# SwiGLU gate and up projections as seven Strassen block products, with SBUF regions by phase

## The chip, the cores and the metric

One core of one Trainium2 chip runs the kernel. The metric is device time in microseconds (us) for one call. The engines are TensorE (PE, with its weight loads PEld), VectorE (DVE), ScalarE (ACT), GpSimd (POOL) and SyncE (SP, which only issues DMAs here).

## The reference

One decoder layer over 512 tokens of 1024 features, in float32. Two feed-forward blocks (FFNs, width 2816) stand around a mixer; a gated per-layer embedding (PLE) and a final norm follow:

```python
def swiglu(x, w_gate, w_up, w_down):
    return (jax.nn.silu(x @ w_gate) * (x @ w_up)) @ w_down
...
    h = h + 0.5 * swiglu(rmsnorm(h, ffn1_norm[i]), ffn1_w_gate[i], ffn1_w_up[i], ffn1_w_down[i])
    n = rmsnorm(h, mix_norm[i])
    proj = n @ w_in[i]
    ...
    h = h + jnp.concatenate([ya, yb], axis=-1) @ w_out[i]
    h = h + 0.5 * swiglu(rmsnorm(h, ffn2_norm[i]), ffn2_w_gate[i], ffn2_w_up[i], ffn2_w_down[i])
    gate = jax.nn.sigmoid(rmsnorm(h, ple_norm[i]) @ ple_w_gate[i] + ple_b_gate[i])
    h = h + gate * (p[i] @ ple_w_proj[i])
return rmsnorm(h, final_norm)
```

## The kernel before

Activations lie in SBUF with features on the 128 partitions and the 512 tokens along the free axis. A weight unit is 128 x 1024: 128 output features, eight contraction tiles. Every float32 product is three float32r passes (`passes`, L151 to L153): weights and activations are each split into a rounded part `hi` and a rest `lo`, and hi*hi + hi*lo + lo*hi accumulate in PSUM. A unit is loaded by SP (`raw`, four buffers), its `hi` is written by ACT (L121, tile `whi`, three buffers) and its `lo` by DVE (L122, `wlo`, three buffers). So a unit costs 24 matmuls of 128 x 512, one ACT cast and one DVE subtraction.

An FFN (`swiglu`) goes through its 22 tiles of width in parts of 8, 7 and 7. In each part every tile has one gate unit and one up unit (48 matmuls). Its results are multiplied by the token's norm factor `r` on DVE, silu on ACT, the product on POOL (L252), and the split for the next projection by ACT (L135) and POOL (L136). Then eight down units, one for each of eight feature tiles of `h`, accumulate that part, and DVE adds them to `h` (L275). After the last part, tile by tile, ACT and DVE make the operand of the next stage (`scaled_split`, L143, L144), and ACT and POOL add the squares for the next norm (L193, L194). The norm's factor commutes with a projection and is worked out behind the first products.

At the start the tiles of `x` and quarter units of the first two weights arrive in turn, and the first products follow tile by tile. The PLE projection (`emb`, L718 to L726, 48 matmuls from `p`) stands between the mixer's output projection and FFN2.

All tiles come from one SBUF pool with a number of buffers for each tag. A scheduler in the language's tile layer sets the order on each engine when the kernel is built; every engine then works through its own list in order, and waits where a row's operands or buffers are not ready.

## Time and profile before

| what | value |
|---|---|
| time, median of 3 runs | 1152.52 us (1152.34 to 1154.45) |
| profiled execution, first to last instruction | 1151.7 us; beside that span no other time of it is recorded, and the median lies 0.8 us above it |
| PE busy | 1134.0 us, 98% of the span |
| DVE, ACT, POOL busy | 605.6, 418.2, 255.2 us |
| granted TensorE clock | 0.998 on the mean |
| gate and up units of both FFNs | 88 units, 2112 matmuls of 128 x 512 |

"Busy" of PE is the union of overlapping matmuls, so the spacing of their starts, not their duration, says what one costs. In a row of a group the numbers behind the bar are busy us and mean ns of one instruction, then the idle time just before it and what ended it.

### The profile page before, as it was taken

Reading aid. Unit: us, or ns where it says so; the run is one execution under the profiler, and the core shown is the slowest. Engines: PE = TensorE matmul, PEld = TensorE weight load, DVE = VectorE, ACT = ScalarE, POOL = GpSimd, SP = SyncE. Lnnn points to the kernel's source line nnn. Section 1 sums busy time; section 2 is a strip of 40 time slices with the busy share of each in tenths; the row PEclk is TensorE's granted clock in tenths of the full one; section 3 lists DMA queues with packets and bytes.
Section 4 is the critical chain, followed back from the end, with each engine's and each line's share of the span. In section 5 each row is a group of like instructions: output and inputs, shape, how many; then the busy total and the mean of one; then the engine's idle time right before and its main releaser. Section 6 shows DMA issues by size and latency. Waiting matters only on the chain.

```text
span 1151.7 us, 13083 instructions
## 1 busy us (share of the span) xinstructions
PE 1134.0 (98%) x5190; PEld 931.2 (81%) x5190; DVE 605.6 (53%) x771; ACT 418.2 (36%) x551; POOL 255.2 (22%) x182
## 2 busy tenths in 40 slices
PE   8999999999999999989999999999999999999997
PEld 6888888888888887777888888888888888888887
DVE  7544344434444688898585734444434443444465
ACT  6322222222234564334543434432212222223455
POOL 1320012101213003675403221032001210121312
PEclk9999999999999999999999999999999999999999
DMA  7233222332233223343332232223322223223311
GB/s 241 92 104 98 92 92 87 96 110 92 87 96 109 92 94 100 128 131 118 128 105 79 73 110 92 92 92 110 92 92 96 92 88 110 95 89 91 110 37 74
DMA packets 36620, 115.29 MB, mean 100 GB/s; under 512 B 4176, under 2 KB 5456, under 8 KB 36560
## 3 DMA queue, kind: packets, MB, share of 16 engines
q1 hardware_dynamic: 32112, 106.97, 28.7%
q10 hardware_dynamic: 4448, 7.50, 2.2%
q8 instruction: 40, 0.66, 0.2%
q14 instruction: 20, 0.16, 0.1%
HBM read 112.29 MB, written 2.16 MB: 99 GB/s over the span
## 4 chain that ended last, share of the span: by engine, by line
PE 89%; DVE 4%; ACT 2%; DMA 1%; issue 1%; POOL 1%; SPq 0%; DVEq 0%; ACTq 0%; POOLq 0%
PE mm L151 29%; PE mm L153 29%; PE mm L152 29%; DMA u<-cs_dram 1%; PE sm L658 1%; DVE wlo L122 1%; DVE tmp L745 1%; POOL xs L530 1%; PE mm L508 0%; DVE u L492 0%; ACT tmp L744 0%; PE sm L203 0%; DMA h<-in_x 0%; DVE h L746 0%; POOL xs L519 0%
## 5 line engine op out<-in xcount | busy, mean ns | idle before, releaser
L152 PE MATMUL mm<-x,whi 128*128 128x512 f32 x1032 | 403.1, 391 | 1.6 <-DVE x L144 1.6
L153 PE MATMUL mm<-x,wlo 128*128 128x512 f32 x1032 | 402.9, 390 | 1.7 <-DVE wlo L122 1.7
L151 PE MATMUL mm<-x,whi 128*128 128x512 f32 x1032 | 404.3, 392 | 0.0
L121 ACT CAST whi<-raw 128x1024 fp32r<-128x1024 f32 (+2 forms) x204 | 205.1, 1008 | 531.1 <-PE mm L152 398.7
L122 DVE TENSOR_TENSOR wlo<-raw,whi 128x1024 fp32r<-128x1024 f32 (+2 forms) x204 | 278.7, 1368 | 72.1 <-ACT whi L121 66.2
L152 PEld LDWEIGHTS mm<-x,whi 128*128 128x128 f32 x1032 | 194.0, 188 | 43.2 <-DVE x L144 3.8
L153 PEld LDWEIGHTS mm<-x,wlo 128*128 128x128 f32 x1032 | 193.9, 188 | 43.1 <-DVE wlo L122 2.5
L151 PEld LDWEIGHTS mm<-x,whi 128*128 128x128 f32 x1032 | 194.1, 188 | 39.6 <-ACT whi L121 0.3
L151 PE MATMUL mm<-yb,whi 128*128 128x512 f32 x416 | 164.6, 396 | 0.0
L153 PE MATMUL mm<-yb,wlo 128*128 128x512 f32 x416 | 164.4, 395 | 0.0
L152 PE MATMUL mm<-yb,whi 128*128 128x512 f32 x416 | 164.4, 395 | 0.0
L252 POOL TENSOR_TENSOR u<-u,xs 128x512 f32<-128x512 f32 x38 | 52.7, 1386 | 502.4 <-DVE u L251 431.3
L275 DVE SCALAR_TENSOR_TENSOR h<-mm,h 128x512 f32<-128x512 f32 x48 | 33.2, 693 | 132.2 <-PE mm L153 132.2
L251 DVE TENSOR_TENSOR u<-mm,rall 128x512 f32<-128x512 f32 x44 | 30.4, 691 | 137.1 <-PE mm L153 137.1
L194 POOL TENSOR_TENSOR ssum<-ssum,tmp 128x512 f32<-128x512 f32 x37 | 57.1, 1542 | 187.5 <-ACT tmp L193 187.4
L153 PEld LDWEIGHTS mm<-yb,wlo 128*128 128x128 f32 x416 | 78.1, 188 | 18.9
L152 PEld LDWEIGHTS mm<-yb,whi 128*128 128x128 f32 x416 | 78.1, 188 | 18.8
L151 PEld LDWEIGHTS mm<-yb,whi 128*128 128x128 f32 x416 | 78.2, 188 | 18.7
L248 DVE TENSOR_TENSOR xs<-mm,rall 128x512 f32<-128x512 f32 x44 | 30.4, 691 | 101.0 <-PE mm L153 101.0
L136 POOL TENSOR_TENSOR yb<-u,yb 128x512 fp32r<-128x512 f32 x38 | 56.3, 1482 | 26.4 <-ACT yb L135 26.4
L135 ACT CAST yb<-u 128x512 fp32r<-128x512 f32 x44 | 27.3, 622 | 58.0 <-POOL u L252 49.6
L249 ACT ACTIVATE xs<-xs 128x512 f32<-128x512 f32 x44 | 27.7, 630 | 1.5 <-DVE xs L248 1.1
(195 smaller groups left out, 856.7 us busy)
## 6 DMA issues: line engine op xcount, KB each, us to landing
raw<-in_ffn_gu SPq DMA_DIRECT2D x86, 512.0 KB, 3.5
raw<-in_w_in SPq DMA_DIRECT2D x29, 512.0 KB, 3.5
raw<-in_ffn_down SPq DMA_DIRECT2D x32, 448.0 KB, 3.3
raw<-in_ffn_down SPq DMA_DIRECT2D x16, 512.0 KB, 3.5
raw<-in_w_out SPq DMA_DIRECT2D x16, 512.0 KB, 3.5
u<-cs_dram ACTq DMA_DIRECT2D x16, 256.0 KB, 3.6
raw<-in_w_v SPq DMA_DIRECT2D x8, 512.0 KB, 3.6
raw<-in_ple_gate SPq DMA_DIRECT2D x8, 512.0 KB, 3.5
```

The source lines that it names most:

```text
L121: nc.scalar.copy(self.hi[:, c], self.raw[:, c])
L122: nc.vector.tensor_tensor(self.lo[:, c], self.raw[:, c], self.hi[:, c].bitcast(F32), ALU.subtract)
L136: (lo_engine or nc.gpsimd).tensor_tensor(lo, src, hi.bitcast(F32), ALU.subtract)
L151: nc.tensor.matmul(ps, whi, xhi, start=first, stop=False)
L152: nc.tensor.matmul(ps, whi, xlo, start=False, stop=False)
L153: nc.tensor.matmul(ps, wlo, xhi, start=False, stop=last)
L194: self.engines[i].tensor_tensor(self.totals[i], self.totals[i], sq, ALU.add)
L248: nc.vector.tensor_tensor(gate, ps[0], r, ALU.mult)
L249: nc.scalar.activation(gate, gate, AF.Silu)
L251: nc.vector.tensor_tensor(up, ps[1], r, ALU.mult)
L252: engine.tensor_tensor(up, up, gate, ALU.mult)
L275: nc.vector.scalar_tensor_tensor(h[d], p_, 0.5, h[d], ALU.mult, ALU.add)
```

## The change

Gate and up weights of both FFNs go through one Strassen-like scheme. The contraction is halved (features 0 to 511 and 512 to 1023), the tokens are halved (2 x 256), and the two column halves of the weight are up and gate. So the product of the 2 x 2 blocks of weights with the 2 x 2 blocks of tokens takes seven block products in place of eight. A group covers two tiles of width; there are 11 groups in an FFN, in parts of 4, 4 and 3.

For each group four quarter-weight tiles of 128 x 1024 are loaded (`raw`: w21 and w11; `rawb`: w22 and w12). POOL makes four combined weights from them: s1 = w21 + w22, s2 = s1 - w11 (both tag `sum`), w11 - w21 in place of w21, and s2 - w12 in place of w12. All seven (three plain, four combined) are split into `whi` and `wlo` by ACT and DVE. Seven products, in the order 1, 6, 2, 7, 5, 4, 3, have 24 matmuls of 128 x 256 each and write three PSUM tiles. DVE adds them up (u2, u3, tag `pu`, and three further sums, tag `q`), multiplies the gate by `r`, ACT takes silu, POOL multiplies by `r` once more, and DVE makes the product `g`. ACT and POOL split `g` into `ghi` and `glo` of 128 x 1024.

The activations are combined once for each FFN by `x_forms`: from two feature tiles of `h` (tile d and tile d + 4) seven blocks of 256 tokens, with their hi and lo parts in one tile `xf`. The order of feature tiles becomes 0, 4, 1, 5, 2, 6, 3, 7 (`D_ORDER`). In an FFN's first group products 1, 6 and 5 go pair by pair (`by_pair`).

Buffers: `raw` 4 to 3, `tmp` 5 to 3, `u` 10 to 8, `ssum` 3 to 2. Two regions, left and right, are released and allocated anew at FFN1, mixer, FFN2 and PLE; a tile of a new region waits for the tiles that lay in its place. At the start `x` is loaded whole by ACT's DMA queue. The PLE projection moves behind FFN2.

```diff
-F_PARTS = (8, 7, 7)
+F_PARTS = (8, 8, 6)
...
+BUFS = {
+    "raw": 3, "whi": 3, "wlo": 3, "tmp": 3, "h": 8, "ssum": 2, "rall": 2, "rtok": 2,
+    "nv": 2, "ny": 2, "nt": 2, "rhi": 2, "rlo": 2, "bnst": 2, "rlast": 2,
+    "xf": 4, "F": 1, "x": 16, "xs": 8, "u": 8, "emb": 8, "pe": 6,
+    "ghi": 4, "glo": 4, "g": 1, "q": 4, "pu": 3, "sum": 2, "rawb": 3, "ya": 16, "yb": 16, "convin": 2, "o": 8,
+}
...
+    def open_region(side, name):
+        if region[side] is not None:
+            region[side].release()
+        region[side] = tc.alloc_tile_pool(name=name, bufs=1, side=side, reuse_waits="tile")
...
+    def x_forms(h0, c0, h1, c1):
+        f = sb("F", (P, 8, HT))
+        xf = sb("xf", (P, 7, 2, HT), F32R)
+        for t, c, i in ((h0, c0, X11_), (h1, c1, X21_)):
+            nc.scalar.activation(f[:, i : i + 2].rearrange("p s t -> p (s t)"), t, AF.Copy, scale=c)
+        nc.vector.tensor_tensor(
+            f[:, T3_ : T1_ + 1],
+            f[:, X22_ : X11_ + 1],
+            f[:, X12_].unsqueeze(1).to_broadcast([P, 2, HT]),
+            ALU.subtract,
+        )
+        nc.vector.tensor_tensor(f[:, T2_], f[:, X22_], f[:, T1_], ALU.add)
+        nc.vector.tensor_tensor(f[:, T4_], f[:, X21_], f[:, T2_], ALU.subtract)
+        nc.scalar.copy(xf[:, :, 0], f[:, :7])
+        nc.vector.tensor_tensor(xf[:, :, 1], f[:, :7], xf[:, :, 0].bitcast(F32), ALU.subtract)
+        return xf
...
+    def w_forms(src, order):
...
+        w21, w22, w11, w12 = (sb(tag, (P, 1024)) for tag in ("raw", "rawb", "raw", "rawb"))
+        for t, i in ((w21, 2), (w22, 3), (w11, 0), (w12, 1)):
+            nc.sync.dma_start(t, src[i])
+        s1 = sb("sum", (P, 1024))
+        s2 = sb("sum", (P, 1024))
+        nc.gpsimd.tensor_tensor(s1, w21, w22, ALU.add)
+        nc.gpsimd.tensor_tensor(s2, s1, w11, ALU.subtract)
+        for i in order:
+            if i == 7:
+                nc.gpsimd.tensor_tensor(w21, w11, w21, ALU.subtract)
+            if i == 3:
+                nc.gpsimd.tensor_tensor(w12, s2, w12, ALU.subtract)
+            yield w_split({1: w11, 2: w12, 3: w12, 4: w22, 5: s1, 6: s2, 7: w21}[i])
...
+    def strassen(src, xfs, by_pair=False):
...
+        def product(ps, i, w, fresh, pairs=range(len(xfs))):
+            whi, wlo = w
+            for p in pairs:
+                for m in range(2):
+                    c = slice((2 * p + m) * P, (2 * p + m + 1) * P)
+                    o = ps[:, m * HT : (m + 1) * HT]
+                    xhi, xlo = xfs[p][:, SLOT[i], 0], xfs[p][:, SLOT[i], 1]
+                    last = p == len(xfs) - 1 and m == 1
+                    for n, (wt, xt) in enumerate(((whi, xhi), (whi, xlo), (wlo, xhi))):
+                        nc.tensor.matmul(
+                            o, wt[:, c], xt, start=fresh and p == m == n == 0,
+                            stop=last and n == 2, skip_group_check=True,
+                        )
...
+        first = (1, 6, 5) if by_pair else (1, 6)
+        rest = (2, 7, 4, 3) if by_pair else (2, 7, 5, 4, 3)
+        forms = w_forms(src, first + rest)
+        x, y, z = (mm_ps() for _ in range(3))
+        if by_pair:
+            ws = [next(forms) for _ in first]
+            for p in range(len(xfs)):
+                for ps, i, w in zip((x, y, z), first, ws):
+                    product(ps, i, w, True, (p,))
+        else:
+            product(x, 1, next(forms), True)
+        p1, u2, u3 = (sb("pu") for _ in range(3))
+        nc.scalar.copy(p1, x)
+        if not by_pair:
+            product(y, 6, next(forms), True)
+        nc.vector.tensor_tensor(u2, y, p1, ALU.add)
+        product(x, 2, next(forms), False)
+        yield "11", halves(x), None, None
+        product(y, 7, next(forms), False)
+        nc.vector.tensor_tensor(u3, y, p1, ALU.add)
+        if not by_pair:
+            product(z, 5, next(forms), True)
+        yield "22", halves(z), halves(u3), ALU.subtract
+        product(y, 4, next(forms), False)
+        yield "21", halves(y), halves(p1), ALU.add
+        product(z, 3, next(forms), False)
+        yield "12", halves(z), halves(u2), ALU.subtract
...
+    def swiglu(h, xfs, norm, w_gu, w_down, closed, after=lambda d: None):
...
+        def group(j):
+            nonlocal tok, r
+            q = {}
+            g = sb("g", (P, 2, T))
+            up = None
+            for which, ps, other, op in strassen(w_gu[j], xfs, by_pair=tok is None):
+                if tok is None:
+                    tok = norm.per_token(D)
+                if which == "11":
+                    up = ps
+                    continue
+                if r is None:
+                    r = Norm.on_all(tok)
+                half = slice(0, HT) if which[1] == "1" else slice(HT, T)
+                t = sb("q", (P, 2, HT))
+                if op == ALU.add:
+                    nc.vector.tensor_tensor(t, ps, other, op)
+                else:
+                    nc.vector.tensor_tensor(t, other, ps, op)
+                if which == "12":
+                    nc.vector.tensor_tensor(g[:, :, half], t, q["2"], ALU.mult)
+                    continue
+                rh = r[:, half].unsqueeze(1).to_broadcast([P, 2, HT])
+                nc.vector.tensor_tensor(t, t, rh, ALU.mult)
+                nc.scalar.activation(t, t, AF.Silu)
+                nc.gpsimd.tensor_tensor(t, t, rh, ALU.mult)
+                q[which[1]] = t
+                if which == "21":
+                    nc.vector.tensor_tensor(g[:, :, half], up, t, ALU.mult)
+            hi = sb("ghi", (P, 2, T), F32R)
+            lo = sb("glo", (P, 2, T), F32R)
+            nc.scalar.copy(hi, g)
+            nc.gpsimd.tensor_tensor(lo, g, hi.bitcast(F32), ALU.subtract)
+            return [(hi[:, m], lo[:, m]) for m in range(2)]
...
+            g = []
+            for j in range(f0 // 2, (f0 + nf) // 2):
+                g += group(j)
+            last = part == len(F_PARTS) - 1
+            if last:
+                closed()
+            for n, d in enumerate(D_ORDER):
                 w = weights(w_down[part][:, d, :], nf * P)
                 p_ = mm_ps()
                 accumulate(p_, w, 0, g)
                 nc.vector.scalar_tensor_tensor(h[d], p_, 0.5, h[d], ALU.mult, ALU.add)
-                if part == len(F_PARTS) - 1:
+                if last:
                     after(d)
                     out_norm.add(h[d])
             f0 += nf
         return out_norm
...
+    def former(name, xfs):
+        def done(d):
+            if d >= NP:
+                xfs.append(x_forms(h[d - NP], col(name, d - NP), h[d], col(name, d)))
+        return done
...
+    h = [None] * ND
+    x_ffn1 = []
+    ffn1 = former("ffn1_norm", x_ffn1)
     norm = Norm(nc.gpsimd, nc.vector)
-    for t in h:
-        norm.add(t)
+    for d in D_ORDER:
+        h[d] = sb("h")
+        nc.scalar.dma_start(h[d], a["x"][:, d, :])
+        ffn1(d)
+        norm.add(h[d])
     x_mix = []
     norm = swiglu(
-        h, x, norm, w_gu, down_units("ffn1_down"), started=ps, after=splitter("mix_norm", x_mix)
+        h, x_ffn1, norm, a["ffn1_gu"], down_units("ffn1_down"),
+        lambda: open_region("left", "mix_left"), splitter("mix_norm", x_mix),
     )
...
+    open_region("right", "mix_right")
...
+    out_ps = [None] * ND
+    for n, d in enumerate(D_ORDER[:AHEAD]):
+        out_ps[d] = mm_ps()
...
+                ya.append(split(u[i], "ya", (nc.vector, nc.gpsimd)[i % 2]))
+    open_region("left", "ffn2_left")
+    for n, d in enumerate(D_ORDER):
+        if n >= AHEAD:
+            out_ps[d] = mm_ps()
             half_out(d, out_ps[d], 1, yb, True, False)
         half_out(d, out_ps[d], 0, ya, False, True)
         nc.vector.tensor_tensor(h[d], out_ps[d], h[d], ALU.add)
-        w_ffn2(d)
+        ffn2(d)
         norm.add(h[d])
...
+    open_region("right", "ffn2_right")
+    x_ple = []
+    norm = swiglu(
+        h, x_ffn2, norm, a["ffn2_gu"], down_units("ffn2_down"),
+        lambda: open_region("left", "ple_left"), splitter("ple_norm", x_ple),
+    )
...
+    pe = []
+    for k in range(2):
+        t = sb("pe")
+        nc.scalar.dma_start(t, a["p"][:, k, :])
+        pe.append(split(t, "pe"))
     emb = []
     for q in range(2):
```

Where rows stand. Names carry a tag and two running numbers.

**A steady group, POOL.** Before, two tiles of width are four rows of 128 x 512:

```order
L252 TENSOR_TENSOR u_85_417<-u_85_417,xs_84_414 128x512
L136 TENSOR_TENSOR yb_87_421<-u_85_417,yb_86_420 128x512
L252 TENSOR_TENSOR u_97_489<-u_97_489,xs_96_486 128x512
L136 TENSOR_TENSOR yb_99_493<-u_97_489,yb_98_492 128x512
L252 TENSOR_TENSOR u_109_561<-u_109_561,xs_108_558 128x512
L136 TENSOR_TENSOR yb_111_565<-u_109_561,yb_110_564 128x512
```

Now one group's time on POOL has s1, w11 - w21, the previous group's `glo`, s2, the two products with `r`, and s2 - w12. The rows here end with a group that no other follows in its part:

```order
L306 TENSOR_TENSOR sum_148_926<-raw_144_918,rawb_145_919 128x1024
L310 TENSOR_TENSOR raw_144_918<-raw_146_920,raw_144_918 128x1024
L407 TENSOR_TENSOR glo_107_673<-g_76_438,ghi_106_672 128x1024
L307 TENSOR_TENSOR sum_149_927<-sum_148_926,raw_146_920 128x1024
L400 TENSOR_TENSOR q_131_839<-q_131_839,rall_66_361 128x512
L400 TENSOR_TENSOR q_134_872<-q_134_872,rall_66_361 128x512
L312 TENSOR_TENSOR rawb_147_921<-sum_149_927,rawb_147_921 128x1024
L407 TENSOR_TENSOR glo_139_911<-g_108_676,ghi_138_910 128x1024
```

L306 and L307 make s1 and s2 of the next group, L310 and L312 the two in-place forms, L407 a `glo`, L400 the products with `r`. Rows of 128 x 512 gave way to rows of 128 x 1024, more of them.

**The same place, DVE.** Before, two tiles of width:

```order
L122 TENSOR_TENSOR wlo_139_715<-raw_137_713,whi_138_714 128x1024
L248 TENSOR_TENSOR xs_132_702<-mm_124_640,rall_63_299 128x512
L122 TENSOR_TENSOR wlo_143_746<-raw_141_744,whi_142_745 128x1024
L251 TENSOR_TENSOR u_133_705<-mm_128_671,rall_63_299 128x512
L122 TENSOR_TENSOR wlo_150_786<-raw_148_784,whi_149_785 128x1024
L248 TENSOR_TENSOR xs_144_774<-mm_136_712,rall_63_299 128x512
```

Now, about one group:

```order
L296 TENSOR_TENSOR wlo_98_574<-sum_84_450,whi_97_573 128x1024
L296 TENSOR_TENSOR wlo_101_607<-rawb_81_443,whi_100_606 128x1024
L357 TENSOR_TENSOR pu_90_484<-mm_78_440,pu_88_482 128x512
L296 TENSOR_TENSOR wlo_104_642<-rawb_83_445,whi_103_641 128x1024
L392 TENSOR_TENSOR q_99_601<-pu_90_484,mm_79_441 128x512
L398 TENSOR_TENSOR q_99_601<-q_99_601,rall_66_361 128x512
L296 TENSOR_TENSOR wlo_119_693<-raw_114_682,whi_118_692 128x1024
L390 TENSOR_TENSOR q_102_634<-mm_78_440,pu_88_482 128x512
L398 TENSOR_TENSOR q_102_634<-q_102_634,rall_66_361 128x512
L296 TENSOR_TENSOR wlo_124_725<-sum_117_689,whi_123_724 128x1024
L403 TENSOR_TENSOR g_76_438<-mm_77_439,q_102_634 128x2x256
L392 TENSOR_TENSOR q_105_669<-pu_89_483,mm_79_441 128x512
```

L296 is a split of weights, L357 u3, L392 and L390 sums from PSUM, L398 the product with `r`, L403 `g`. Seven splits stand where four stood, and sums stand between them.

**The start, PE.** Before, behind nine warming matmuls:

```order
L97 MATMUL sm_7_77<-tmp_6_75 128x512 x9
L151 MATMUL mm_15_96<-x_18_106,whi_10_91 128x512
L152 MATMUL mm_15_96<-x_19_107,whi_10_91 128x512
L153 MATMUL mm_15_96<-x_18_106,wlo_11_92 128x512
L151 MATMUL mm_16_97<-x_18_106,whi_13_94 128x512
```

Now the sum of squares for the norm (L231), which needs all eight tiles of `x`, stands behind the second product matmul:

```order
L125 MATMUL sm_7_83<-tmp_6_81 128x512 x9
L330 MATMUL mm_34_171<-xf_13_103,whi_43_186 128x256 x2
L231 MATMUL sm_54_304<-ones_4_77,ssum_10_98 128x1 x4
L330 MATMUL mm_35_172<-xf_13_103,whi_45_190 128x256 x2
L330 MATMUL mm_34_171<-xf_13_103,wlo_44_187 128x256
L330 MATMUL mm_34_171<-xf_13_103,whi_43_186 128x256 x2
L330 MATMUL mm_34_171<-xf_13_103,wlo_44_187 128x256
```

**The start of FFN2.** Before, the PLE projection (its moving operand is a tile `xs`) followed the mixer's output on PE:

```order
L151 MATMUL mm_940_5194<-x_880_4801,whi_945_5226 128x512
L152 MATMUL mm_940_5194<-x_881_4802,whi_945_5226 128x512
L153 MATMUL mm_940_5194<-x_880_4801,wlo_946_5227 128x512
L151 MATMUL mm_953_5269<-xs_842_4664,whi_951_5264 128x512
L152 MATMUL mm_953_5269<-xs_843_4665,whi_951_5264 128x512
```

Now the first products follow at once, and product 6, which needs s2 (tile whi_1028), comes after 19 matmuls of product 1 and the norm's sum:

```order
L330 MATMUL mm_1017_6298<-xf_996_6143,whi_1026_6313 128x256 x2
L330 MATMUL mm_1017_6298<-xf_996_6143,wlo_1027_6314 128x256
L330 MATMUL mm_1017_6298<-xf_996_6143,whi_1026_6313 128x256 x2
L330 MATMUL mm_1017_6298<-xf_996_6143,wlo_1027_6314 128x256
L231 MATMUL sm_1037_6430<-ones_4_77,ssum_967_5924 128x1 x4
L330 MATMUL mm_1017_6298<-xf_1014_6282,whi_1026_6313 128x256
L330 MATMUL mm_1018_6299<-xf_972_5958,whi_1028_6317 128x256 x2
L330 MATMUL mm_1017_6298<-xf_1014_6282,whi_1026_6313 128x256
```

SP loads w22 and w12 of this group (rawb_1021 and rawb_1023) with waits for PE, since the mixer's operands lay in their place:

```order
L303 DMA raw_1020_6301<-in_ffn2_gu 128x1024 [waits DMAHW4_49,DVE_49]
L303 DMA raw_1022_6303<-in_ffn2_gu 128x1024 [waits DMAHW5_49,DVE_49]
L303 DMA raw_1063_6568<-in_ffn2_gu 128x1024 [waits DMAHW6_49,DVE_49]
L303 DMA rawb_1021_6302<-in_ffn2_gu 128x1024 [waits PE_49,Pool_49]
L303 DMA rawb_1023_6304<-in_ffn2_gu 128x1024 [waits PE_49,Pool_49]
```

217 lines of the change are left out of this document (93 added, 124 removed).

## The prediction

> **What bounds the kernel now.** I read the page's busy line and the shares of the chain that ended last first, since they say which engine sets the end:
>
> ```profile
> PE 1134.0 (98%) x5190; PEld 931.2 (81%) x5190; DVE 605.6 (53%) x771; ACT 418.2 (36%) x551; POOL 255.2 (22%) x182
> PE 89%; DVE 4%; ACT 2%; DMA 1%; issue 1%; POOL 1%; SPq 0%; DVEq 0%; ACTq 0%; POOLq 0%
> ```
>
> TensorE carries the chain. The windows by stage show where it waits (after the window: its length, then busy us of PE, PEld, DVE, ACT, POOL, the granted clock, DMA share and GB/s):
>
> ```profile
> 0.00:20.00 20.00, 16.73 (x56) 11.66 (x57) 14.18 (x26) 14.63 (x29) 5.29 (x10) 1.00 0.77 247
> 32.50:330.00 297.50, 297.50 (x1304) 244.47 (x1303) 124.90 (x116) 81.50 (x97) 53.51 (x37) 1.00 0.30 95
> 400.00:500.00 100.00, 96.56 (x490) 77.31 (x489) 84.94 (x131) 48.89 (x65) 35.98 (x26) 1.00 0.37 118
> 600.00:720.00 120.00, 120.00 (x553) 99.30 (x553) 61.63 (x75) 44.64 (x60) 28.85 (x18) 1.00 0.27 88
> 1080.00:1120.00 40.00, 40.00 (x180) 32.97 (x179) 22.01 (x35) 20.20 (x27) 9.27 (x6) 1.00 0.21 66
> ...
> 1148.00:1152.00 4.00, 0.00 (x0) 0.00 (x0) 0.00 (x0) 0.00 (x0) 0.00 (x0) 0.50 0.58 224
> ```
>
> In FFN1 (32.5 to 330) PE never stops, DVE works 42% and POOL 18%. The ways into FFN2 (600 to 720) and PLE (1080 to 1120) show no gap. Only the start and the mixer do. So matmuls that go are worth their pace, and everything the change adds to DVE and POOL must stay under PE's cover.
>
> **Removed: matmuls.** The pace is the distance of starts. The timeline of PE, first and last row of each kind (an operand `x`, an operand `yb`, and the 256-token products near the end):
>
> ```profile
> 1094.18 0.39 PE L151 MATMUL mm<-x,whi 128*128 128x512 f32 x1
> ...
> 1096.22 0.39 PE L151 MATMUL mm<-x,whi 128*128 128x512 f32 x1
> ...
> 135.03 0.39 PE L151 MATMUL mm<-yb,whi 128*128 128x512 f32 x1
> ...
> 139.93 0.40 PE L151 MATMUL mm<-yb,whi 128*128 128x512 f32 x1
> ...
> 1128.06 0.28 PE L152 MATMUL sm<-x,whi 128*128 128x256 f32 x1
> ...
> 1134.54 0.28 PE L152 MATMUL sm<-x,whi 128*128 128x256 f32 x1
> ```
>
> Nine steps in 2.04 us are 0.2267 us, 21 steps in 4.90 us are 0.2333, and 54 steps in 6.48 us are 0.1200. Before, 2112 x 0.2267 = 479 us. Now 22 groups x 168 x 0.1200 = 443.5 us. **Term: -35 us.** If the combined operand paced like `yb`, 3% slower, it would be -22. An eighth of the work goes, but half-length matmuls cost 53% of whole ones, so half the nominal 60 us is lost at once.
>
> The Trainium skill, "TensorE: Matmul & The Clock Gate", section Wait — 56ns, not 53.3ns?, gives a warm start-to-start of N / 2.4 GHz plus about 2.5 ns: 109 ns for 256 columns. By that estimate the new products would take 404 us. The trace disagrees: 120.0 ns, so the row decides.
>
> **Added: port work in a steady group.** How long POOL and DVE take, and what happens when they meet:
>
> ```profile
> 209.02 1.09 DVE L122 TENSOR_TENSOR wlo<-raw,whi 128x896 fp32r<-128x896 f32 x1
> ...
> 209.06 2.20 POOL L252 TENSOR_TENSOR u<-u,xs 128x512 f32<-128x512 f32 x1 [7.36 <-ACT whi L121]
> 211.99 1.29 POOL L136 TENSOR_TENSOR yb<-u,yb 128x512 fp32r<-128x512 f32 x1 [0.73 <-ACT yb L135]
> ...
> 668.59 1.22 DVE L122 TENSOR_TENSOR wlo<-raw,whi 128x1024 fp32r<-128x1024 f32 x1 [0.21 <-ACT whi L121]
> ...
> 669.19 1.78 POOL L194 TENSOR_TENSOR ssum<-ssum,tmp 128x512 f32<-128x512 f32 x1 [8.81 <-ACT tmp L193]
> ```
>
> The groups by shape (busy us, mean ns of one):
>
> ```profile
> L790 POOL TENSOR_TENSOR ssum<-ssum,tmp 128x256 f32<-128x256 f32 x4 | 2.9, 736 | 9.4 <-ACT tmp L749 9.4
> L251 DVE TENSOR_TENSOR u<-mm,rall 128x512 f32<-128x512 f32 x44 | 30.4, 691 | 137.1 <-PE mm L153 137.1
> L122 DVE TENSOR_TENSOR wlo<-raw,whi 128x1024 fp32r<-128x1024 f32 x164 | 239.4, 1461 | 69.4 <-ACT whi L121 66.2
> L121 ACT CAST whi<-raw 128x1024 fp32r<-128x1024 f32 x164 | 171.9, 1050 | 434.4 <-PE mm L152 324.0 <-issue 105.9 <-PE mm L153 4.1
> L249 ACT ACTIVATE xs<-xs 128x512 f32<-128x512 f32 x44 | 27.7, 630 | 1.5 <-DVE xs L248 1.1
> ```
>
> A POOL operation that starts just behind a DVE operation on two SBUF tiles takes 2.20 or 1.78 us where one alone takes 1.29: DVE's ends at 210.11, and 1.15 us later POOL's does; 669.81 and 1.16 us likewise. So the two take turns. Sums that read PSUM (L251) do not enter this, as I choose from their even 691 ns.
>
> 128 x 256 takes 0.736 and 128 x 512 takes 1.29, so another 256 elements take 0.555, and a 128 x 1024 POOL form is estimated at 1.29 + 2 x 0.555 = 2.40 us. One group puts on POOL four forms and one `glo` (5 x 2.40) and two products with `r` (2 x 1.29): 14.6 us. DVE has seven splits (7 x 1.22) and three 512-wide operations on SBUF tiles (3 x 0.69): 10.6 us. Each of these seventeen holds its turn about 0.14 us less than it lasts (1.29 less 1.15): 14.6 + 10.6 - 17 x 0.14 = 22.8 us of turns in a frame for which PE needs 168 x 0.120 = 20.2 us. DVE has six sums from PSUM besides, 6 x 0.69 = 4.1 us, that run beside POOL only where POOL has work just then. Hidden wholly the frame is 22.8, not at all 26.9. By the order of rows POOL is idle beside u3 and one `q` sum, as the next form's buffer (`sum` has two) comes free only behind a split; I take two of the six: **24.2 us, 4.0 over PE**.
>
> A frame counts as full where the part has a group before it and one after: two in a part of four, one in a part of three. I add 0.9 us for the part's other frames, and give the first part, whose first group is a term of its own and makes no forms ahead for the second, 6. Per FFN 6 + 8.9 + 4.9 = 19.8. **Term: +40 us**; with frames of 22.8 it is 26, of 26.9 it is 67, and with free ports nothing. ACT stays out of it: 7 x 1.05, 2 x 0.63 and 2 x 1.05 are 10.7 us.
>
> **Part ends.** Before the down units can finish they need the last group's `g`: after its last product the sums, ghi (1.05) and `glo` (2.40) behind the port turns of the first down splits (1.6), with 2.9 us from silu, POOL's product and the sums: 8.0 us. PE's cover is six earlier tiles, 18 x 0.2333 = 4.2 us, and 0.7 of drain: 4.9; in a part of three groups 3.5. Four ends at 3.1 and two at 4.5 give 21. **Term: +20** (10 if silu's chain is done earlier, 26 if each step waits a turn). Before, the last `glo` was 1.29 and the window from 32.5 shows no gap there.
>
> **Start of FFN1.** The first 32.5 us before, in the timeline of PE:
>
> ```profile
> 1.66 4.21 PE L97 MATMUL sm<-tmp 128*128 128x512 f32 x9 [1.66 <-DVE tmp L94]
> ...
> 32.43 0.39 PE L153 MATMUL mm<-x,wlo 128*128 128x512 f32 x1
> ```
>
> Two tiles of width were done at 32.5, the same as a group; x (2.1 MB) and weights shared the queue. Now 4.2 MB must land before the last products' operands exist: at 247 GB/s 17 us. `x_forms` then is a chain over one `F` buffer: two scaled ACT copies (2 x 0.72, the 0.62 of a plain one below and 0.1 for the scale, an estimate), three DVE sums (0.69 + 2 x 0.4), the 1792-wide cast (1.05 x 1.75 = 1.84) and remainder (1.22 x 1.75 = 2.1), 6.9 us a pair, 27.6 for four. From the first pair's landing at 7 or 8 us and with three weight splits between (3.7) the last pair is ready at about 38. Behind it come its 18 matmuls and four products, 114 x 0.120 = 13.7, and about 4 for splits behind u2 and the factor's sum L231, which stands at the head of PE's list and needs all of x: 56 us. Of the old 32.5, 1.6 are already in the first term: 56 - 30.9, **term +25** (17 if the casts run ahead, 32 if norm adds take turns).
>
> **Starts of FFN2 and PLE.** From `h` to the norm's sum (timeline at the mixer's end; last, the issue of `p`, KB each and us to landing):
>
> ```profile
> 717.15 0.69 DVE L713 TENSOR_TENSOR h<-mm,h 128x512 f32<-128x512 f32 x1
> ...
> 718.54 0.62 ACT L193 ACTIVATE tmp<-h 128x512 f32<-128x512 f32 x1
> ...
> 719.31 1.49 POOL L194 TENSOR_TENSOR ssum<-ssum,tmp 128x512 f32<-128x512 f32 x1 [9.93 <-ACT tmp L193]
> ...
> xs<-in_p SPq DMA_DIRECT2D x2, 256.0 KB, 3.0
> ```
>
> The PLE projection's 48 matmuls, 48 x 0.2267 = 10.9 us, covered this and are now gone from here. POOL's list has L194, then s1 and s2, which product 6 needs split: 0.69 + 0.62 + 1.49 + 2 x 2.40 + 1.05 + 1.22 = 9.9 and about 2 of turns with the last `x_forms`, 12 us. PE has product 1, 24 x 0.120 = 2.9. **Term: +9** (5 if s1 is formed before L194's operand, 13). Before PLE the sum L231 waits the same chain without forms, 0.69 + 0.62 + 1.49 and a turn of 1.2, 4 us, and the loads of `p`, issued behind it on ACT's queue, land 3.0 later: **+6** (3 to 10).
>
> **Mixer and clock.** The chain of waits already holds loads of rows into `u`:
>
> ```profile
> 452.43 3.94 DMA u<-cs_dram
> ...
> 493.17 5.69 DMA u<-cs_dram
> ```
>
> `u` has eight buffers for ten, `tmp` three for five, so these loads start later where nothing else moves: zero to three such loads, **+4** (0 to 12). The clock was 0.50 in the last window, where PE stood; and nine warming matmuls took 4.21 us in place of 9 x 0.2267 = 2.04. A restart costs 2.2 us; two long waits (FFN1, FFN2) give **+4** (0 to 8). The Trainium skill, "TensorE: Matmul & The Clock Gate", section What's actually happening, says that an idle window of about 3.4 us halves the clock until as long a busy one has passed. By that estimate each restart costs some 1.7 us, and every stall over that length would pay it. The last window agrees; the part ends, at 3 to 4.5 us, would be on the edge.
>
> **Sum.** -35 + 40 + 20 + 25 + 9 + 6 + 4 + 4 = +73 on the execution's 1151.7 us, which is 0.8 under the median: **1225 us**.
>
> **Rivals.**
> A, the turns do not bind: PSUM sums, DMA landings and ACT hide them and frames run at PE's 20.2. For it: DVE has only 42% before; against it: 22.8 is a sum of whole operations. Without the 40 and with part ends at 12: 1151.7 - 35 + 12 + 25 + 9 + 6 + 4 + 4 = 1177.
> B, faster: the same with forms made ahead through the down units, so that part ends vanish and starts cost half (20): 1151.7 - 35 + 20 = 1137. It decides as soon as all stalls stay under 35 us, 1.6 per group. For it: 48 down units leave POOL free; against: `sum` has two buffers and `raw` three, less than one group ahead.
> C, each DVE operation, PSUM sums too, waits out a POOL operation: frames of 26.9 (+27 on the 40), part ends at 26 (+6), starts at 32, 13 and 10 (+15): 1225 + 48 = 1273. For it: L122's mean is already 1.46 us for 1.22 alone, with little POOL work.
>
> **Chances.** Forecast 0.72, A 0.14, B 0.08, C 0.06. The forecast's own bounds are about 1195 to 1255; with A's time nearly at its edge and C's beyond, 8 in 10 lie in 1168 to 1265. Faster by over 0.2% (what the runs can tell from no change) is B and a bit of A: 0.09; within it 0.02; slower 0.89.
>
> **What would show it.** PE pitch of 0.120 in the products; POOL rows of 128 x 1024 near 2.4 us, longer behind DVE; groups about 24 us apart in the middle of a part, with PE idle before products 7 and 4 released by DVE splits; gaps of 3 to 5 us at part ends released by `glo`; the first group done near 56 us; about 9 us idle at FFN2's start. Groups 20 us apart would refute the turns (A or B), a first group done by 40 the term for FFN1, and a POOL form of 1.3 us the price.

## The result, and the profile after

The changed kernel takes 1258.03 us (median of 4 runs, 1256.0 to 1259.4) against 1152.58 us before: ratio 1.091, 95% interval 1.0895 to 1.0926. It is slower by 105 us; 1225 was predicted, in a range of 1168 to 1265. The profiled execution has a span of 1253.9 us, 102.2 more than that of before.

The busy line and the clock of the page of after:

```profile
PE 1135.8 (91%) x6774; PEld 993.6 (79%) x6774; DVE 890.8 (71%) x945; ACT 505.1 (40%) x619; POOL 533.8 (43%) x260
...
PEclk6799999999999999999999999798999999999899
```

PE is busy for as long as before (1134.0) with an eighth of the gate and up work gone, and idle for 118.1 us instead of 17.7. DVE has gained 285 us and POOL 279. Where PE waited, by the engine and tile that ended the wait (us in total, times, longest):

```profile
PE mm L330 <- ACT pu L350: 36.5, 14, 3.0
PE mm L330 <- ACT whi L295: 20.1, 3, 18.1
PE mm L330 <- ACT xf L288: 10.5, 3, 5.8
PE mm L179 <- ACT ghi L406: 6.7, 6, 1.6
PE mm L180 <- POOL glo L407: 6.6, 6, 1.3
PE mm L330 <- DVE pu L357: 6.4, 9, 2.1
PE sm L231 <- POOL ssum L222: 5.4, 2, 4.0
```

The prediction's terms put against the stages of both traces. Each limit is the start or end of a stage's matmuls; "predicted" is the same terms summed by stage, with the matmul term shared out by group and the clock term half to each FFN's first group:

| stage | before, us | after, us | difference | predicted |
|---|---|---|---|---|
| start to the end of the first two tiles of width | 32.7 | 67.9 | +35.2 | +25.4 |
| rest of FFN1 | 340.8 | 361.4 | +20.6 | +14 |
| mixer | 343.5 | 346.7 | +3.2 | +4 |
| FFN2's first two tiles | 23.2 | 39.3 | +16.1 | +9.4 |
| rest of FFN2 | 340.8 | 361.5 | +20.7 | +14 |
| PLE with `p`'s projection (11.2 before) | 70.8 | 77.1 | +6.3 | +6 |

**A steady group.** One stop in the trace's timeline, with the rows of PE that only go on left out:

```profile
94.54 1.22 DVE L296 TENSOR_TENSOR wlo<-rawb,whi 128x1024 fp32r<-128x1024 f32 x1
...
94.79 0.28 PE L330 MATMUL mm<-xf,wlo 128*128 128x256 f32 x1
95.67 0.69 DVE L394 TENSOR_TENSOR g<-q,q 128x512 f32<-128x512 f32 x1
95.89 2.69 POOL L312 TENSOR_TENSOR rawb<-sum,rawb 128x1024 f32<-128x1024 f32 x1 [2.59 <-issue]
96.27 3.39 DVE L296 TENSOR_TENSOR wlo<-raw,whi 128x1024 fp32r<-128x1024 f32 x1
96.39 1.04 ACT L406 CAST ghi<-g 128x1024 fp32r<-128x1024 f32 x1 [2.83 <-DVE g L394]
97.34 0.58 ACT L350 COPY pu<-mm 128x512 f32<-128x512 f32 x1
...
97.98 0.51 PE L330 MATMUL mm<-xf,whi 128*128 128x256 f32 x2 [2.90 <-ACT pu L350]
98.32 0.28 PE L330 MATMUL mm<-xf,wlo 128*128 128x256 f32 x1
98.45 0.45 PE L330 MATMUL mm<-xf,whi 128*128 128x256 f32 x2
98.66 3.25 POOL L306 TENSOR_TENSOR sum<-raw,rawb 128x1024 f32<-128x1024 f32 x1
```

Products 1 and 6 are done; product 2 adds to the PSUM tile that p1 has to be copied from, and that 0.58 us copy on ACT stands behind the last group's `ghi`, which waits for `g`, which is late on DVE. The split at 96.27 takes 3.39 us for 1.22 of its own: it waits out POOL's form, which itself began behind `g`. The windows around this stop (columns as in the prediction):

```profile
92.00:95.00 3.00, 3.00 (x26) 2.85 (x24) 1.82 (x4) 1.57 (x2) 1.30 (x1) 1.00 0.01 4
95.00:98.00 3.00, 0.10 (x2) 0.03 (x1) 3.00 (x3) 1.61 (x3) 2.11 (x1) 1.00 0.00 0
98.00:101.00 3.00, 3.00 (x16) 3.00 (x17) 3.00 (x3) 0.87 (x1) 2.92 (x2) 0.61 0.16 23
101.00:104.00 3.00, 3.00 (x24) 3.00 (x23) 2.33 (x2) 1.05 (x1) 2.92 (x2) 0.82 0.44 152
```

While PE stands, DVE is busy all the time. Behind the stop the clock falls to 0.61, and 16 matmuls go through where 26 did. That is not what makes the group long: the third group of the next part stops for 2.99 us, keeps its clock, and takes 24.4 us all the same.

```profile
228.00:252.40 24.40, 20.34 (x170) 19.61 (x169) 23.14 (x17) 9.81 (x12) 19.06 (x8) 1.00 0.29 87
```

DVE is busy for 23.14 of these 24.40 us.

**How the turns stretch both engines.** The groups of weights' splits and of POOL's forms:

```profile
L296 DVE TENSOR_TENSOR wlo<-rawb,whi 128x1024 fp32r<-128x1024 f32 x66 | 133.8, 2030 | 10.4 <-ACT whi L295 10.2
...
L407 POOL TENSOR_TENSOR glo<-g,ghi 128x1024 fp32r<-128x1024 f32 x22 | 68.1, 3094 | 24.7 <-ACT ghi L406 24.7
...
L306 POOL TENSOR_TENSOR sum<-raw,rawb 128x1024 f32<-128x1024 f32 x22 | 65.7, 2988 | 85.8 <-DMA raw<-in_ffn_gu 70.4 <-DVE nv L197 7.2 <-DMA rawb<-in_ffn_gu 4.7
...
L398 DVE TENSOR_TENSOR q<-q,rall 128x512 f32<-128x512 f32 x44 | 52.4, 1191 | 1.4
...
L392 DVE TENSOR_TENSOR q<-pu,mm 128x512 f32<-128x512 f32 x44 | 29.9, 679 | 3.4 <-PE mm L330 3.3
```

A split that takes 1.22 us by itself took 2.03 on the mean, a form 2.99. By the times of the single operations, the 75 splits of L296 that began with a POOL operation under way took 2.92 us on the mean, and the other 79 took 1.22. L398, with both operands in SBUF, is stretched likewise. The sums that read one operand from PSUM, as L392 does, are not: 62 of them began with a POOL operation under way, and each took 0.67 to 0.69 us.

**The starts.** FFN1's, from the timelines of POOL, DVE and PE:

```profile
13.07 2.35 POOL L307 TENSOR_TENSOR sum<-sum,raw 128x1024 f32<-128x1024 f32 x1
15.37 2.80 POOL L310 TENSOR_TENSOR raw<-raw,raw 128x1024 f32<-128x1024 f32 x1
...
15.88 4.16 DVE L289 TENSOR_TENSOR xf<-F,xf 128x1792 fp32r<-128x1792 f32 x1
...
23.96 0.80 PE L330 MATMUL mm<-xf,whi 128*128 128x256 f32 x2 [18.09 <-ACT whi L295]
...
46.22 2.03 DVE L289 TENSOR_TENSOR xf<-F,xf 128x1792 fp32r<-128x1792 f32 x1 [1.81 <-ACT xf L288]
```

A form alone takes 2.35 us, as worked out (2.40). The first pair's remainder takes 4.16 us beside POOL, the last pair's 2.03 alone. The four pairs of `x_forms` go from 8.3 to 48.3 us, one after the other over the single F. FFN2's longest stop and the one ahead of PLE:

```profile
784.19 0.58 PE L330 MATMUL mm<-xf,whi 128*128 128x256 f32 x1 [3.48 <-ACT xf L288]
...
1181.03 1.87 PE L231 MATMUL sm<-ones,ssum 128*128 128x1 f32 x8 [3.99 <-POOL ssum L222]
```

### The profile page after: what moved, and what is told of

Read it like the earlier page. It is cut to its first block, busy times and chain, and to the rows that moved or that the text cites. A ratio compares the mean times of both kernels' runs of the same rounds, so it can differ in the third digit from the quotient of the medians.

```text
span 1253.9 us, 16693 instructions
## 1 busy us (share of the span) xinstructions
PE 1135.8 (91%) x6774; PEld 993.6 (79%) x6774; DVE 890.8 (71%) x945; ACT 505.1 (40%) x619; POOL 533.8 (43%) x260
## 5 line engine op out<-in xcount | busy, mean ns | idle before, releaser
L330 PE MATMUL mm<-xf,whi 128*128 128x256 f32 x2464 | 459.6, 290 | 82.5 <-ACT pu L350 36.5
L330 PEld LDWEIGHTS mm<-xf,whi 128*128 128x128 f32 x2464 | 395.9, 199 | 93.1 <-ACT pu L350 39.3
L330 PE MATMUL mm<-xf,wlo 128*128 128x256 f32 x1232 | 355.9, 289 | 2.2 <-DVE wlo L296 2.0
L330 PEld LDWEIGHTS mm<-xf,wlo 128*128 128x128 f32 x1232 | 243.9, 198 | 4.7 <-DVE wlo L296 4.1
L150 DVE TENSOR_TENSOR wlo<-raw,whi 128x1024 fp32r<-128x1024 f32 (+1 forms) x110 | 141.3, 1286 | 35.9 <-ACT whi L149 35.3
L180 PE MATMUL mm<-glo,whi 128*128 128x512 f32 x352 | 141.0, 401 | 6.6 <-POOL glo L407 6.6
L179 PE MATMUL mm<-ghi,whi 128*128 128x512 f32 x352 | 139.4, 398 | 6.7 <-ACT ghi L406 6.7
L296 DVE TENSOR_TENSOR wlo<-rawb,whi 128x1024 fp32r<-128x1024 f32 x66 | 133.8, 2030 | 10.4 <-ACT whi L295 10.2
L181 PE MATMUL mm<-ghi,wlo 128*128 128x512 f32 x352 | 138.8, 395 | 0.0
L400 POOL TENSOR_TENSOR q<-q,rall 128x512 f32<-128x512 f32 x44 | 66.2, 1503 | 126.5 <-ACT q L399 125.1
L181 PE MATMUL mm<-x,wlo 128*128 128x512 f32 x264 | 104.6, 396 | 1.8 <-DVE wlo L150 1.8
L179 PE MATMUL mm<-x,whi 128*128 128x512 f32 x264 | 106.2, 402 | 0.0
L180 PE MATMUL mm<-x,whi 128*128 128x512 f32 x264 | 104.3, 395 | 0.0
L312 POOL TENSOR_TENSOR rawb<-sum,rawb 128x1024 f32<-128x1024 f32 x22 | 57.5, 2613 | 106.6 <-DVE wlo L296 65.2
L306 POOL TENSOR_TENSOR sum<-raw,rawb 128x1024 f32<-128x1024 f32 x22 | 65.7, 2988 | 85.8 <-DMA raw<-in_ffn_gu 70.4
L296 DVE TENSOR_TENSOR wlo<-raw,whi 128x1024 fp32r<-128x1024 f32 x44 | 94.1, 2139 | 7.4 <-ACT whi L295 7.4
L296 DVE TENSOR_TENSOR wlo<-sum,whi 128x1024 fp32r<-128x1024 f32 x44 | 87.0, 1978 | 1.1 <-ACT whi L295 0.8
```

Source lines behind the costliest of these rows:

```text
L150: nc.vector.tensor_tensor(self.lo[:, c], self.raw[:, c], self.hi[:, c].bitcast(F32), ALU.subtract)
L179: nc.tensor.matmul(ps, whi, xhi, start=first, stop=False)
L180: nc.tensor.matmul(ps, whi, xlo, start=False, stop=False)
L181: nc.tensor.matmul(ps, wlo, xhi, start=False, stop=last)
L296: nc.vector.tensor_tensor(lo, raw, hi.bitcast(F32), ALU.subtract)
L306: nc.gpsimd.tensor_tensor(s1, w21, w22, ALU.add)
```

## The experiments

Times are medians of the runs; single ones are said to be single. "Profile" is the profiled execution's span, to be set beside 1253.9 of the changed kernel.

### Product 5 ahead of product 2

```diff
-        first = (1, 6, 5) if by_pair else (1, 6)
-        rest = (2, 7, 4, 3) if by_pair else (2, 7, 5, 4, 3)
+        first = (1, 6, 5)
+        rest = (2, 7, 4, 3)
...
             product(y, 6, next(forms), True)
+            product(z, 5, next(forms), True)
```

> Products in the order 1, 6, 5, 2, 7, 4, 3 in every group; nothing else. Queue theory: the changed kernel stops before product 2 because the copy of p1 (0.58 us on ACT) stands behind the last group's ghi, which waits for g; with product 5 ahead of product 2 that wait of 2.9 us in ten groups and 1.7 to 2.0 in four is covered, and the half clock behind the long ones goes too: groups of 20 to 21 us, 1200 to 1215 us. Port theory (the prediction's): the turns of DVE and POOL set 22.8 to 24.2 us a group wherever PE stops, so the stop moves to another product and the time stays at 1240 to 1258.

Measured: 1293.24 us, ratio to before 1.1226 (1.1205 to 1.1247); worse than either theory had it. The wait moved and grew:

```profile
PE mm L330 <- DVE pu L358: 79.6, 19, 7.0
```

L358 is u3 here. In this order nothing stands between product 7, which u3 reads, and product 4, which writes over the same PSUM tile, so PE waits for DVE to get to u3, up to 7.0 us. The wait for the copy of p1 is gone. The groups in the middle of a part take 27 to 28 us instead of 21 to 24, while the last ones take 20 to 21 instead of 24 to 26. The queue of ACT was where PE happened to stop, not why. The run also says that I had priced the edit without its own cost: a cover taken from one wait was needed at another.

### Idle matmuls in the stop

```diff
+        if fill:
+            spare = sm_ps()
+            for n in range(fill):
+                nc.tensor.matmul(spare[:, :HT], ones_r, xfs[3][:, 0, 0], start=True, stop=True)
         product(x, 2, next(forms), False)
```

> The changed kernel with 16 idle matmuls of 128 x 256 (1.9 us, their result unused) between products 6 and 2 of seven groups of each FFN, those that stopped there. They fit into the wait. Clock theory: the wait of 2.9 us halves the clock for some 3 us after it, 1.65 to 1.9 us lost in ten groups; with PE kept at work the clock stays and the time falls by 15 to 20 us, to about 1240, with the wait for the copy ending at the same place. If the clock costs nothing there: 1258 within 3, or a few us more where the matmuls are in the way (four groups wait only 1.7 to 2.0).

Measured: 1245.17 us (1.0793, 1.0777 to 1.081), 13 less than the changed kernel, for more work. The wait for the copy falls by what the fill covers:

```profile
PE mm L330 <- ACT pu L350: 14.1, 10, 3.0
```

From the starts of the product matmuls I summed what those 130 to 260 ns apart take over 116 ns, the mark of the half clock: 29.5 us in the changed kernel, 15.1 here. Some 10 of these 14 us lie in the last groups of the six parts, and those groups became 12 us shorter together. The third groups took 24.3 to 24.4 us in the changed kernel, two with 1.8 and 2.0 us of half clock and two with 0.6 or less. Here the three with 0.6 or less take 24.2 to 24.4, and the one that kept more (2.8) takes 25.6. So up to 2 us of half clock did not show in a full group, whose length the turns set, while it cost time in the groups that no other follows. The other 4 to 5 us lie in the first groups, which had no fill.

### Without the four combined weights, in both orders

```diff
-        nc.gpsimd.tensor_tensor(s1, w21, w22, ALU.add)
-        nc.gpsimd.tensor_tensor(s2, s1, w11, ALU.subtract)
...
-            if i == 7:
-                nc.gpsimd.tensor_tensor(w21, w11, w21, ALU.subtract)
-            if i == 3:
-                nc.gpsimd.tensor_tensor(w12, s2, w12, ALU.subtract)
-            yield w_split({1: w11, 2: w12, 3: w12, 4: w22, 5: s1, 6: s2, 7: w21}[i])
+            yield w_split({1: w11, 2: w12, 3: w12, 4: w22, 5: w21, 6: w22, 7: w21}[i])
```

> The four combined weights are not formed: POOL's four operations of 128 x 1024 per group are left out, and plain weights are split in their place, so the output is not the reference's. Port theory: POOL's turns fall from 14.6 to 5.0 us a group, groups run at PE's 20 us, no stop before product 2, about 1205. Queue theory: the chain sum, r, silu, r, g, sum, g, ghi, copy of p1 loses only its 1.5 to 2 us of turns of its 8.7 against 5.8 of cover, so a stop of 0.8 to 1.5 us stays before product 2, without the half clock: groups of 21, about 1215.

> Both edits: the order 1, 6, 5, 2, 7, 4, 3, and the four combined weights left out (the output is not the reference's). Queue theory: steady groups within 0.3 us of the ones with the new order alone, so the forms then cost at the starts and part ends only, 5 to 15 us in all. Port theory: groups fall by 2.5 us or more against the new order alone, 25 us or more in all.

Measured, one run each: 1168.72 us (profile 1167.0), and 1185.82 (1184.1) with the new order. The busy line of the first:

```profile
PE 1102.9 (95%) x6774; PEld 967.8 (83%) x6774; DVE 744.5 (64%) x945; ACT 509.8 (44%) x619; POOL 259.2 (22%) x172
```

and its wait for the copy of p1:

```profile
PE mm L322 <- ACT pu L342: 4.2, 11, 0.4
```

DVE executes the same 945 instructions and is busy for 744.5 us where it was 890.8: 146 us of its time had been waiting for POOL's 88 forms. Groups take 19.0 to 20.2 us, and 0.4 us is the longest wait for the copy of p1, so the queue theory's remaining stop of 0.8 to 1.5 is refuted. The time is 36 us below the 1205 that I had expected by the port theory: the twenty groups behind the first ones lose 67 us together, and the starts shrink too, which it did not name. The first group ends at 57.0 us, FFN2's takes 28.7. With the new order the forms cost 102 us (1286.3 to 1184.1), against the 5 to 15 of the queue theory; what stays there is 0.85 us a group before product 4 (17.0 us in 20 waits), the price of the order itself.

### The combined weights on DVE

```diff
-        nc.gpsimd.tensor_tensor(s1, w21, w22, ALU.add)
+        nc.vector.tensor_tensor(s1, w21, w22, ALU.add)
```

and likewise for the other three.

> The changed kernel with its four combined weights made on DVE in place of POOL, nothing else. Left out, they took the profile from 1253.9 to 1167.0 us. Turn theory (DVE and POOL exclude each other): a form on POOL holds 2.35 us, on DVE 1.22, so the turns of a group fall from 22.8 to 5.0 + 8.5 + 2.1 + 4.9 less 0.14 each = 18.3 us, and DVE's whole list is 19.6: groups of 20 to 21.5 us against 24.3, 1195 to 1215 us. Theory that POOL was only a second pair of hands whose own list was too long: DVE, now with the longer list, becomes the bound at 19.6 plus 5 us of POOL's own operations, 24 us and more, 1250 us or longer.

Measured: 1199.24 us (1.0398, 1.038 to 1.0417), as the turns have it. The same splits, and a form, now on DVE:

```profile
L296 DVE TENSOR_TENSOR wlo<-rawb,whi 128x1024 fp32r<-128x1024 f32 x66 | 80.9, 1226 | 6.8 <-ACT whi L295 6.4
...
L306 DVE TENSOR_TENSOR sum<-raw,rawb 128x1024 f32<-128x1024 f32 x22 | 44.5, 2021 | 20.7 <-DMA raw<-in_ffn_gu 15.5 <-DMA rawb<-in_ffn_gu 5.0
```

These splits are back at 1.23 us, and DVE, with 88 operations more, is busy for less time (857.7 against 890.8 us). The form shown takes 2.02 us, as it meets POOL's `glo`; the other three take 1.22, and it does too once `glo` has left POOL (the last step below). Groups take 19.0 to 22.4 us, two of them 24.

### First groups without Strassen

```diff
+                for k, slot in enumerate((X11_, X21_)):
+                    whi, wlo = split_ws[k]
+                    for m in range(2):
+                        c = slice((2 * p + m) * P, (2 * p + m + 1) * P)
+                        for n, (wt, part) in enumerate(((whi, 0), (whi, 1), (wlo, 0))):
+                            for tok in range(2):
+                                nc.tensor.matmul(
+                                    out[tok][:, m * HT : (m + 1) * HT], wt[:, c], xf[:, slot + tok, part],
...
+            if row == 0:
+                for _, forms in xfs:
+                    forms()
```

> The changed kernel, but the first group of each FFN is computed without Strassen (192 matmuls of 128 x 256 on the plain parts of x, up before gate, pair by pair); the loads of x stand between those of the first weights on SP's queue; the combined operands are made behind the first half of these products, in four blocks (F holds four). Rest as changed (q two buffers for four, convin one for two, to make room). Theory of the starts: what PE waits for is the chain of x_forms over one F and, in FFN2, s1 and s2 behind the norm; so the first group ends at 36 to 42 us in place of 67.9, FFN2's takes 23 to 26 in place of 39.3: 1210 to 1218. Rival: the forming is DVE work that has to be done anyway, and the wait turns up before group 1: less than 20 us gained, over 1235.

Measured, one run: 1220.41 us (profile 1218.7), between the theories. The first group ends at 46.3 us instead of 67.9 and FFN2's takes 23.6 instead of 39.3; but group 1 waits some 5 us for u2 in each FFN and takes 28.7 and 27.1 where it took 21.2 and 21.7. 37 us came off, 13 came back: in part the work was only put off. The span fell by 35 us and not by 24; the rest came off later groups, such as group 2 of each FFN (21.3 and 21.4 us instead of 24.3), and why was not tried.

### All remedies together, and parts of it undone

Beside the two above, r leaves POOL and is applied behind the down projection, the last group of a part is given cover, and `p` is loaded and projected within FFN2's last part:

```diff
-                nc.gpsimd.tensor_tensor(t, t, rh, ALU.mult)
...
+            for d in D_ORDER[:2]:
+                w = weights(w_down[part][:, d, :], nf * P)
+                begun.append((w, mm_ps()))
+                accumulate(begun[-1][1], w, 0, g[:-2], True, False)
...
-                nc.vector.scalar_tensor_tensor(h[d], p_, 0.5, h[d], ALU.mult, ALU.add)
+                s = tmp()
+                nc.vector.scalar_tensor_tensor(s, p_, 0.5, r, ALU.mult, ALU.mult)
+                nc.vector.tensor_tensor(h[d], s, h[d], ALU.add)
```

> All remedies together: forms on DVE, plain first groups, the factor r taken out of POOL's product and put on the down projection's results, the loads and the projection of p moved into FFN2's last part, and the first two down outputs begun on the earlier groups' g. Without stops an FFN is 23 + 10 x 19.1 + 123 = 337 us of PE against 364 before. Turn theory: groups of 20 to 20.5 us, part ends under 1 us, start at 40 or below: 1130 to 1155, at or under the kernel before. If DVE's 18 to 20 us a group cannot be hidden: groups of 22 and 1165 to 1180.

Measured: 1131.86 us, ratio to before 0.9812 (0.9794 to 0.9831): 1.9% less than before, the first version below it. Groups take 19.1 to 20.9 us, part ends show no stop, PLE takes 59.9 us behind FFN2 as before the change (59.6).

Two single steps undone in it, the forms and the product with r:

> The version with all remedies, but its four combined weights are made on POOL again. Turn theory: POOL 5 x 2.35 and DVE 8.5 + 2.1 us less 0.14 each make 20.7 us of turns, with 4 us of sums from PSUM that meet POOL only partly: groups of 21.5 to 22.5 us against 20.3, profile 1150 to 1175 against 1127. Rival: dropping POOL's product with r and the plain first groups already took the pressure off, within 10 us of 1127.

> The version with all remedies, but the second product with r stays on POOL in each group (2 x 1.29 us) and not on the down projection's results. Turn theory: 2.3 us of turns more a group and a longer chain to g, groups of 20.8 to 21.5 us, 1135 to 1150. If it lies in the shade: 1127 within 4.

And the third, a further step:

```diff
-            nc.gpsimd.tensor_tensor(lo, g, hi.bitcast(F32), ALU.subtract)
+            nc.vector.tensor_tensor(lo, g, hi.bitcast(F32), ALU.subtract)
```

> The version with all remedies, with glo on DVE too, so that POOL does nothing in the groups. DVE's list becomes 19.6 + 1.2 = 20.8 us a group, over PE's 19.1, but no turn is left to wait for (glo on POOL holds 2.35). If turns count as much as the list: 20.3 to 20.9 a group, the same time within 5 us of 1132; if DVE's list is what binds, 8 to 12 us slower.

Measured: forms back on POOL 1161.15 us (one run, profile 1159.2); the second product with r back on POOL 1160.27 (one run, 1158.5); `glo` on DVE too 1120.03, ratio 0.9711 (0.9695 to 0.9727). The first is as the turns have it. The second costs 31 us by the profile (1127.1 to 1158.5) for 44 operations of 1.29 us, more than the 8 to 23 I expected, and that although DVE's second operation on each down result goes. That the longer chain to `g` adds to the turns is likely but was not tried by itself. The third is 12 us better than the version it was made from, where I expected the same or worse. Its busy line:

```profile
PE 1097.7 (98%) x6822; PEld 971.2 (87%) x6822; DVE 860.2 (77%) x1099; ACT 504.1 (45%) x626; POOL 147.1 (13%) x110
```

and two windows, of FFN1 and of the middle of its second part:

```profile
32.50:330.00 297.50, 296.89 (x2156) 278.36 (x2155) 244.44 (x281) 125.53 (x138) 0.00 (x0) 1.00 0.33 97
168.00:208.00 40.00, 40.00 (x349) 40.00 (x347) 39.79 (x44) 21.01 (x23) 0.00 (x0) 1.00 0.35 106
```

With no POOL operation in FFN1's groups, DVE is busy 39.79 of 40 us and PE all of them: two full lists beside each other. Groups take 19.0 to 19.8 us, PE's own pace, but for group 1's 20.6.

### The order of loads, and the same kernel without Strassen

Both start from the version with `glo` on DVE. The loads:

```diff
-        if n % 2 == 0:
-            w = load_plain(a["ffn1_gu"][0], n // 2)
-            started.append(w_split(w) if n < 4 else w)
+        if n % 2 == 0 and n < 4:
+            started.append(w_split(load_plain(a["ffn1_gu"][0], n // 2)))
...
+    started += [load_plain(a["ffn1_gu"][0], i) for i in (2, 3)]
```

> The version with glo on DVE, with all tiles of x loaded ahead of the first gate weights. Where the first group (34.0 us for 23 us of matmuls) waits for the landing of x: 2 to 4 us less, 1116 to 1118. Where it waits for DVE, which forms T blocks and meets POOL's norm sums between the plain parts of x: the same within 1.5 us of 1120.

And every group like the first:

```diff
-            parts = strassen(w_gu[j], [xf for xf, _ in xfs])
-            if j == 0:
-                parts = plain(started or [load_plain(w_gu[0], i) for i in range(4)], xfs)
+            parts = plain(j == 0 and started or [load_plain(w_gu[j], i) for i in range(4)], xfs)
```

> The version with glo on DVE, but every group is computed like the first, without Strassen (192 matmuls for 168, eight splits' worth of plain weights instead of seven, no combined weights or operands). If the gain over the kernel before comes from the block products: 20 groups x 24 x 0.1145 = 55 us lost and some DVE time won, 1165 to 1178, above the kernel before. If it comes from the other remedies (order of part ends, r on the down results, loads): within 1% of 1120.

Measured: `x` loaded first 1124.79 us (0.9752, 0.9737 to 0.9766), 4.8 slower, which neither theory had. The first group takes 29.0 us instead of 34.0, and group 1 27.1 instead of 20.6, with DVE busy for 25.6 of the 27.1. So the landing of x did hold up the first group, and DVE's list, with the forming of the combined operands in it, holds up the next one; neither alone sets the start. These two groups explain 1.5 us of the loss; the rest is spread and was not traced. Every group without Strassen: 1174.69 (1.0184, 1.0167 to 1.0201), 54.7 us slower than the same kernel with it. So the gain comes from the block products. The rest of what was changed makes it possible, but is no gain by itself in this form, which is 21 us slower than the kernel before.

## Why the prediction was right, and where it was off

**The direction and the mechanism held.** The turns of DVE and POOL were the main term. Taking the forms away gives groups of 19.0 to 20.2 us, moving them to DVE 19.0 to 22.4 for all but two. Rivals A (1177, no turns) and B (1137) fall with that. C (1273: every DVE operation, sums from PSUM too, waits out a POOL operation) is refuted by the sums from PSUM, which kept their 0.67 to 0.69 us beside POOL.

**The time was less exact than the direction.** 1258 lies beyond the forecast's own bounds of 1195 to 1255, and nearer to C's 1273 than to 1225. It lies in the range because that reached past these bounds, toward C.

**Turns: +40 predicted, 55 measured, and not where I put them.** At the pace that was priced, 20.2 us a group, the twenty groups behind the first ones took 55 us more. The ten that the term counted as full, with a group of their part before and behind them, took 21.2 to 24.4 us, 23.1 on the mean, against 24.2 predicted. What the term had nearly at PE's pace is the last group of each part: these six took 24.2 to 25.6 us, 28 us of the 55. Each stops for 2.9 to 3.0 us ahead of its product 2, for the chain to `g` of the group before, and pays half clock behind it.

**Where PE stops was wrong.** I expected it before products 7 and 4, released by splits on DVE. It was before product 2, released by ACT's copy of p1; in the reordered kernel it was before product 4. I had walked DVE's and POOL's lists and not ACT's, taken off the path at 10.7 us a group. Its busy time was not the matter (9.8 us in a group of 24.4), but an engine that works in order is late as soon as one operation in its list is, however little it has to do.

**Matmuls: -35 predicted, about -53 measured.** The pace of 0.1200 us came from the PLE stretch. The products have 0.1152 on the mean over their undisturbed starts. The rows in which one product begins and, 24 matmuls later, the next:

```profile
185.33 0.39 PE L330 MATMUL mm<-xf,whi 128*128 128x256 f32 x2
...
188.05 0.39 PE L330 MATMUL mm<-xf,whi 128*128 128x256 f32 x2
```

2.72 us for 24 steps is 113.3 ns, half of the 226.7 of a whole matmul, so halving the columns loses nothing here; other products have 117.8. In a full group the faster pace gave little back, as the turns set its length. The Trainium skill, "TensorE: Matmul & The Clock Gate", section Wait — 56ns, not 53.3ns?, gave an estimate of 109 ns; the products lie between it and the row I let decide.

**Clock: +4 predicted, some 32 us of half clock measured.** This amount was the most mis-sized, though not all of it is time of the kernel. Half-clock time is 29.5 us in the products and some 7 in the 512-wide matmuls, against some 4.5 before. I had priced a restart at 2.2 us and counted two. There are 21 stops of over 1.3 us: those of 1.7 to 2.0 us cost 0.1 each, those of 2.9 to 3.0 cost 1.2 to 2.7 in eight of ten and 0.1 in the two others; the seven in the two first groups cost 1.2 to 2.3. With the fill 14 of them went, and the time fell by 13 us, 10 by the profile; most of that came off the last groups of the parts. In the first groups, which have 11 of the 29.5, the cost of the half clock by itself was not tried. The Trainium skill, "TensorE: Matmul & The Clock Gate", section What's actually happening, has a free-running window of about 3.4 us decide; the uneven price of equal stops agrees with that, but no run here shows the window itself.

**FFN1's start: +25 predicted, +35 measured.** 56 us was said, 67.9 it was. The chain over F was right, its length not: 40 us for four pairs, where 27.6 and 3.7 for weights in between were counted. The norm sums on DVE and POOL, the factor's small operations and the turns (4.16 for 2.03) stand between its links; the forms account for 11 us of it (57.0 without).

**FFN2's start: +9 predicted, +16 measured by stage.** The waits for the norm (1.4 us), for the last `x_forms` (3.5), for splits (0.9 and 1.5) and before product 4 (3.1) come one after another, with some 5 us of half clock behind them, which the term had left to the clock. Without the forms it was 28.7 us instead of 39.3.

**Part ends, PLE, mixer: +20, +6, +4 predicted.** The six part ends wait 13.3 us by the table of waits (ACT's ghi, POOL's glo), 2.2 each where gaps of 3 to 5 were said, and each FFN's rest takes 8.7 us more than its groups explain, so about 17. (The term took 20 where its working gives 21, and no row has the 0.7 us of drain in it.) PLE is +6.3, gone when `p` is projected earlier; the mixer is +3.2, and stays at 347 to 349 us in all versions. That the fewer buffers cause it was not tried.

By stages the sum of 73 was 29 short of the 102: 10 at FFN1's start, 7 at FFN2's first group, 13 in the rests of the FFNs, where the last groups of the parts were missed and the part ends came out 3 cheaper.

## What to carry to other kernels

When work moves off TensorE, sum what it puts on engines that exclude each other, in turns, before counting its gain: here some 55 us of matmuls showed as a gain only after the forms and the product with r had left POOL (a form takes 1.22 us on DVE, 2.35 on POOL) and the starts and part ends had been changed too. Moving the forms alone left it at 1199 us. A stop that moves when the order is changed is not caused by the order; take the suspected load away instead. And for each short operation that frees a PSUM tile, look at what stands ahead of it on its own engine, and look for the half clock behind stops of 3 us: it cost time here in the groups that PE had to finish alone, while 2 us of it did not show in those that DVE and POOL set.
